# Three small moves in a hybrid mLSTM and attention layer: sample state operations behind the third value tile, sample value rows in idle strips, one gate-up weight piece in tile space of its own

## The chip, the cores and the metric

The kernel runs on one core of one Trainium2 chip, as one launch. The metric is device time in microseconds (us). The engines are TensorE (PE in the profile; its weight loads are PEld), VectorE (DVE), ScalarE (ACT), GpSimd (POOL) and SyncE (SP), which issues nearly all DMA transfers. Each engine works through its own queue in the order in which its instructions stand there, and waits at an instruction until what that instruction needs has been done elsewhere.

## The reference

One inference step of one decoder layer for two groups with the same weights: a prompt of 512 tokens and a sample group of 8 sequences with one token each. All is fp32.

```python
x = layer_norm(x, ln_in_g, ln_in_b)
z = x @ w_in
qk, mv, mi, mf, mo, aq, ak, av, gm, ga = split(z)
qk, conv_state = causal_dwconv(qk, conv_buf, conv_w, conv_b)        # width 4, silu
mq, mk = split(qk, 2)
h, C, n, m = mlstm_chunkwise(mq, mk, mv, mi + b_igate, mf + b_fgate, C0, n0, m0)
h = h * rsqrt(mean(h*h) + RMS_EPS)                                  # per head
y_m = sigmoid(mo) * h * m_norm_g
y_a, k_win, v_win = window_attention(aq, ak, av, k_buf, v_buf, attn_sinks, start)
mixed = sigmoid(gm) * y_m + sigmoid(ga) * y_a
x = layer_norm(ALPHA * x + mixed @ w_out, ln1_g, ln1_b)
g, u = split(x @ w_gate_up, 2)
ffn = (silu(g) * u) @ w_down
ple = sigmoid(x @ w_ple_gate) * (p @ w_ple)
x = layer_norm(ALPHA * x + ffn + ple, ln2_g, ln2_b)
```

The mLSTM has 4 heads with keys of 128 and values of 256 channels. For a sample token, one step of its recurrence is, for each of the 8 sequences and 4 heads,

```python
C_new = decay_prev * C + w_state * outer(k, v)      # 128 x 256 per sequence and head
n_new = decay_prev * n + w_state * k                # 128 per sequence and head
h     = (C_new^T q) / max(|n_new . q|, exp(-m_new))
```

Every C, n and m of the sample group is read, updated and written out. Attention has 16 query and 2 key-value heads of 64 channels and a window of 128.

## The kernel before, in words

Activations are kept transposed, channels on the 128 partitions and 520 columns for the tokens: 8 sample tokens first, then the 512 of the prompt. A projection is worked in tiles `f` of 128 output channels, and each tile in two halves of 264 and 256 columns, one PSUM bank each. fp32 products are made from a high and a low part, with three matmuls for each: high by high, high by low and low by high (L245, which stands for nearly all projection matmuls). So one tile with 1024 input channels is 48 matmuls of L245.

**Weights** come in blocks by DMA (L165, into one of two `raw` buffers) and are used in pieces of 128 x 1024. `prep_next` splits a piece: ACT copies it rounded, the high part (L218, `whi<-raw`), and DVE subtracts, the low part (L219, `wlo<-raw,whi`). The parts go to two rings of three buffers, `whi` and `wlo`, unless `dest` names another place for the piece. `get` splits up to two pieces ahead of the one in use.

**What sets the order.** Outside of `tc.manual_schedule` blocks a scheduler, which simulates the program, sets the order of every engine's queue; code order, dependences and buffer rings are its input. `after(f, ..., f_=[ins])` tells it to issue what `f` makes behind the instruction `ins`. Inside the `manual_schedule` blocks the queues of PE, DVE, POOL and ACT hold what is written, in the written order.

**The projections** run one tile after another, numbered `t`: the mLSTM queries and keys (`qk`, t 0 to 7), its values (`mv`, from `t_mv` = 8), attention keys and values (from `t_k` = 16), attention queries (`aq`, from `t_aq` = 18), and then the gates `mo`, `gm` and `ga`. After each tile `sd.run(t)` takes steps from the lists of side work: `sd.add(steps, start, end)` spreads a list evenly over the tiles from `start` to `end`. All that is neither a projection nor its eviction is side work. The lists that the change touches or borders on are:

- `conv_out` (L967): transposes the last columns of the convolution, copies them from PSUM to `ost` (L973) and stores them (L974, L975). Before, `ost` is a buffer of the ring `stg` with two buffers.
- `ev_mv(f)` (L981) is the eviction of a value tile. ACT copies the two halves into a `stg` buffer (L984), PE transposes that (L987 for the prompt, L992 for the 8 sample rows), DVE copies the results away (L988, L996), and after each second tile the sample rows go to DRAM, to `vsd` (L998).
- `smlstm_prep` (L1095): prepares the sample step. PE transposes the old `n` (L1099); DVE makes the scaled keys `kws` (L1102, L1103), the new `n` (L1104, L1105, in `nst`) and `qn` (L1106); PE transposes `nst` back (L1109), DVE copies that (L1111) and it is stored (L1113). The decay and input factors `wdb` come by a broadcast from DRAM (L913), behind the gate rows `bcd` (L912).
- `ml0` to `ml3`: the prompt's mLSTM in 4 chunks of 128 for each head. `ml0(h)` loads two rows per head, broadcast over the partitions (L1036, L1037), to the strips 2h and 2h+1, POOL adds a mask to the first (L1040); `ml1` reads them chunk by chunk (L1054 on ACT and a product on POOL). A strip is a 128 x 520 tile, and there is one buffer for each of the eight.
- `sm0`, `sm1`, `sm2`: the sample step, in eight units `(h, g)` of one head and four sequences. `sm0` loads the four 128 x 256 matrices `Ct` (L1120) and the four value rows `vb`, broadcast over the partitions from `vsd` (L1121, 512 KB), each to one of four `big` buffers. `sm1` scales the value rows by the keys (ACT, L1141), adds the decayed state (DVE, L1142), splits the result into high and low for the product with the query (L218 on ACT, L219 on POOL), and stores `Ct` (L1152). The units run skewed: in one step of the list the load of one unit, the work of the one before it, and the end (`sm2`) of the one before that.
- attention (`at1` to `at3`: L684 to L743) runs in the same stretch, from `t_aq` on.

**Gate-up.** After the output projection and its LayerNorm the gate and up projections begin. Their first five pieces, `k_gu` to `k_gu+4`, are split before the LayerNorm's last part; a manual block runs their first-half matmuls between the LayerNorm's steps, and their second half after it. Then come pieces 5 to 7, still of the plain kind, and behind them a Strassen phase (L1580 to L1684) that reads combinations of the activations: `tsum` (L1492 to L1496) and `tsplit` (L218, L219 into `tf`) make these on DVE and ACT in the same stretch.

## Time and profile before

| what | value |
| --- | --- |
| time, median of 3 runs | 886.09 us (884.8 to 888.52) |
| time of the profiled execution | 885.6 us |
| its span | 883.5 us |
| mean granted PE clock in it | 0.995 |
| PE busy | 866.0 us (98%) |
| DVE busy | 659.4 us (75%) |
| ACT busy | 475.5 us (54%) |
| POOL busy | 156.2 us (18%) |
| DMA, mean over the span | 117 GB/s |

The span runs from the first instruction to the last that the profiler recorded; the execution's own time has about 2 us more around it. All positions below are microseconds from the span's start. In a row of the timeline stand the start, the busy time, the engine, the line, the operation, the tile that is written and those that are read, how many instructions were put together in the row (x2), and in brackets how long the engine was idle before it and what released it. A row of windows has the stretch, its length, for PE, PEld, DVE, ACT and POOL the busy time and the number of instructions, and then the granted PE clock (1.00 is full speed), the DMA engines' busy share and GB/s. A row of waits has an engine with the line that waited, what released it, the sum in us, how often, and the longest. DMA-issuing queues are called SPq.

### The profile page before, as it was taken

How to read it: one execution, taken by the hardware profiler on the slowest of the kernel's cores; microseconds unless marked ns; L12 is line 12 of the kernel's file. 1: busy time of each engine (PE TensorE's matmuls, PEld its weight loads, DVE VectorE, ACT ScalarE, POOL GpSimd, SP SyncE). 2: the span in 40 equal slices, each digit the busy share in tenths (PEclk: the TensorE clock that was granted, in tenths of full speed). 3: DMA queues.
4: the chain of work that ended last, by engine and by line, in shares of the span. 5: the costliest groups of instructions: out<-in, count | busy, mean ns of one | idle time of the engine just before them, and what ended most of it. 6: DMA issues, size and time to landing. Idle time of an engine off the chain costs nothing.

```text
span 883.5 us, 18583 instructions
## 1 busy us (share of the span) xinstructions
PE 866.0 (98%) x7082; PEld 853.2 (97%) x7082; DVE 659.4 (75%) x1589; ACT 475.5 (54%) x1131; POOL 156.2 (18%) x315
## 2 busy tenths in 40 slices
PE   8999899999999999999999999999999999999996
PEld 7999899999999899999999999999999999999996
DVE  7788555688978676778876968898898875566337
ACT  6545254658777655566525846666666565222120
POOL 5441321115464411221012300000000000000002
PEclk9999999999999999999999999999999999999998
DMA  7642631336465451131520043333334337634212
GB/s 244 223 145 73 194 102 55 55 106 145 157 180 172 145 143 49 49 97 48 191 97 1 23 111 104 112 108 97 107 101 116 108 115 219 202 120 150 96 37 97
DMA packets 125369, 103.69 MB, mean 117 GB/s; under 512 B 7210, under 2 KB 121090, under 8 KB 125256
## 3 DMA queue, kind: packets, MB, share of 16 engines
q1 hardware_dynamic: 125136, 102.38, 38.7%
q8 instruction: 55, 0.90, 0.4%
q14 instruction: 34, 0.28, 0.1%
q10 hardware_dynamic: 144, 0.13, 0.0%
HBM read 91.14 MB, written 12.47 MB: 117 GB/s over the span
## 4 chain that ended last, share of the span: by engine, by line
PE 87%; DVE 5%; DMA 3%; ACT 2%; issue 1%; POOL 1%; SPq 0%; DVEq 0%; ACTq 0%
PE psm L245 41%; PE psm L1601 14%; PE pss L1601 11%; PE psm L228 5%; PE psm L1894 2%; PE psm L1918 2%; PE pss L684 2%; PE pss L737 1%; PE pss L721 1%; PE psm L1429 1%; DMA big<-vsd 1%; PE psm L468 1%; PE pss L1070 1%; PE pss L1074 1%; DMA wdb<-bcd 1%
## 5 line engine op out<-in xcount | busy, mean ns | idle before, releaser
L245 PE MATMUL psm<-T,whi 128*128 128x264 f32 (+1 forms) x1728 | 301.9, 287 | 0.2 <-ACT th L1169 0.2
L245 PEld LDWEIGHTS psm<-T,whi 128*128 128x128 f32 x1728 | 246.8, 189 | 2.1 <-ACT th L1169 0.5
L245 PE MATMUL psm<-T,wlo 128*128 128x256 f32 (+1 forms) x912 | 200.1, 288 | 1.5 <-DVE wlo L219 1.5
L245 PEld LDWEIGHTS psm<-T,wlo 128*128 128x128 f32 x912 | 145.7, 189 | 2.5 <-DVE wlo L219 1.9
L219 DVE TENSOR_TENSOR wlo<-raw,whi 128x1024 fp32r<-128x1024 f32 (+2 forms) x75 | 90.5, 1207 | 66.8 <-ACT whi L218 66.7
L218 ACT ACTIVATE whi<-raw 128x1024 fp32r<-128x1024 f32 (+2 forms) x75 | 77.2, 1034 | 96.9 <-PE psm L245 79.5
L1784 POOL COPY amaskA<-tmp 128x8 f32<-128x8 f32 x8 | 1.5, 189 | 362.9 <-DVE tmp L1782 362.8
L709 POOL TENSOR_SCALAR g<-g,sm 128x256 f32<-128x256 f32 (+1 forms) x64 | 36.2, 579 | 80.2 <-DVE sm L707 23.8
L1585 DVE TENSOR_TENSOR whi<-raw,whi 128x512 fp32r<-128x512 f32 x55 | 37.8, 688 | 11.6 <-ACT whi L1580 10.7
L1580 ACT ACTIVATE whi<-raw 128x512 fp32r<-128x512 f32 x55 | 34.6, 628 | 19.5 <-PE psm L1601 14.4
L1580 ACT ACTIVATE wlo<-raw 128x512 fp32r<-128x512 f32 x55 | 34.6, 629 | 16.3 <-ACT gt L1619 10.2
L1585 DVE TENSOR_TENSOR wlo<-raw,wlo 128x512 fp32r<-128x512 f32 x55 | 37.8, 687 | 6.0 <-ACT wlo L1580 5.6
L702 ACT ACTIVATE g<-g,sm 128x256 f32<-128x256 f32 (+1 forms) x64 | 30.2, 474 | 18.7 <-DVE sm L698 17.7
L245 PE MATMUL psm<-L,whi 128*128 128x264 f32 x192 | 38.7, 282 | 0.0
L219 POOL TENSOR_TENSOR gt<-big,gt 128x256 fp32r<-128x256 f32 x32 | 27.7, 873 | 51.3 <-ACT gt L218 39.5
L1601 PE MATMUL psm<-tf,whi 128*128 128x260 f32 x276 | 36.7, 282 | 0.0
L1601 PE MATMUL psm<-T,wlo 128*128 128x260 f32 x264 | 35.3, 283 | 0.0
L1601 PE MATMUL pss<-tf,whi 128*128 128x260 f32 x264 | 35.3, 283 | 0.0
L1601 PE MATMUL pss<-tf,wlo 128*128 128x260 f32 x264 | 35.3, 283 | 0.0
L1601 PE MATMUL psm<-T,whi 128*128 128x260 f32 x264 | 35.3, 283 | 0.0
L1601 PEld LDWEIGHTS psm<-tf,whi 128*128 128x128 f32 x276 | 34.5, 188 | 0.0
L1601 PE MATMUL psm<-tf,wlo 128*128 128x260 f32 x252 | 33.5, 282 | 0.0
(461 smaller groups left out, 2104.3 us busy)
## 6 DMA issues: line engine op xcount, KB each, us to landing
raw<-in_w_in_dram SPq DMA_DIRECT2D x24, 1024.0 KB
raw<-in_w_gate_up_dram SPq DMA_DIRECT2D x72, 256.0 KB
raw<-in_w_down_dram SPq DMA_DIRECT2D x8, 1024.0 KB
big<-in_state_mlstm_C_dram SPq DMA_DIRECT2D x8, 512.0 KB
big<-vsd SPq DMA_DIRECT2D x8, 512.0 KB
out_dram<-big SPq DMA_DIRECT2D x8, 512.0 KB
raw<-in_w_out_dram SPq DMA_DIRECT2D x4, 1024.0 KB
raw<-in_w_gate_up_dram SPq DMA_DIRECT2D x4, 1024.0 KB
```

The costliest lines, as they stand in the source:

```text
L218: S.activation(rr(hi), src, AF.Copy)
L219: (le or V).tensor_tensor(rr(lo), src, hi, ALU.subtract)
L228: T.matmul(ps[:, :n], rr(w[:, k, wc : wc + P]), rr(a[k0 + k][:, c0 : c0 + n]), start=(i == 0), stop=(i == tot - 1),)
L245: T.matmul(ps[:, :n], rr(w[:, k, wc : wc + P]), rr(a[k0 + k][:, c0 : c0 + n]), start=(i == 0), stop=(i == tot - 1),)
L684: T.matmul(sc[:, a, :w], rr(q[:, a, n * P : (n + 1) * P]), rr(KS[:, kv, hl, (n - 1 + k0) * P : (n + 1) * P]), start=(hl == 0), stop=(hl == 1),
L702: S.activation(pr[:, a, :w], pr[:, a, :w], AF.Exp, bias=sm[:, 2 + a : 3 + a], scale=ASC, accum_out=sm[:, 8 + a : 9 + a],)
L709: G.tensor_scalar(pr[:, a, :w], pr[:, a, :w], sm[:, 12 + a : 13 + a], 0.5, ALU.mult, ALU.mult)
L1580: S.activation(rr(t[:, 0]), wsrcs[i], AF.Copy)
L1585: V.tensor_tensor(rr(lo), wsrcs.pop(i), hi, ALU.subtract)
L1601: T.matmul(ps[:, :TH], rr(w[:, j, :]), rr(x[j]), start=(start and j == 0 and i == 0), stop=(j == 3 and i == 2), skip_group_check=not start,)
L1894: T.matmul(pA[a][:, :264], rr(w[:, a * P : (a + 1) * P]), rr(x[:, :264]), start=(j == 0 and i == 0), stop=(j == KF - 1 and i == 2),)
L1918: T.matmul(pC[c][:, :256], rr(hk[k][x][:, t0 : t0 + P]), rr(w), start=(k == 0 and i == 0), stop=(k == KF - 1 and i == 2),)
```

## The change

1. `conv_out` takes `ost` from the ring `g2` instead of `stg`.
2. `ev_mv` notes its copy of the transposed values (L988). The three steps of `smlstm_prep` are taken at the tiles `t_mv + 2` and `t_mv + 3` instead of `t_mv` to `t_mv + 2`, and are issued behind that copy, which at that time is the one of the third value tile (f = 2).
3. `sm0` no longer puts the value rows into one `big` buffer with one 512 KB broadcast. It loads two halves of 256 KB, one each to the strips 4 + 2g and 5 + 2g, which hold rows of the mLSTM heads 2 and 3 until their last chunk has been worked. `sm1` reads the rows there.
4. Gate-up piece `k_gu+5` gets a place of its own: 1024 columns at the end of slab 3 (`mx3[0]`) for its high part and of `T5[0]` for its low part, both free until the gated activations are written there. Its split is written into the manual block, behind the activation of piece 4's first half.

```diff
@@ conv_out
-            ost = ring("stg", NT, 2)
+            ost = g2()
@@ ev_mv
-        V.tensor_copy(
+        late_t["mv"] = V.tensor_copy(
             vaug()[:, :, f // 2, (f % 2) * P : (f % 2 + 1) * P], ps.rearrange("p (c d) -> p c d", c=NCH)
-        )
+        ).ins
@@ sm0
-        vb = big()[:, :1024].rearrange("p (b d) -> p b d", b=4)
         nc.sync.dma_start(Ct, st_C[0, 4 * g : 4 * g + 4, h].rearrange("b k d -> k b d"))
-        nc.sync.dma_start(
-            vb, vsd[4 * g : 4 * g + 4, h * DV : (h + 1) * DV].partition_broadcast(P)
-        )
+        vb = []
+        for i in range(2):
+            v2 = strip(4 + 2 * g + i)[:, :512].rearrange("p (b d) -> p b d", b=2)
+            b0 = 4 * g + 2 * i
+            nc.sync.dma_start(v2, vsd[b0 : b0 + 2, h * DV : (h + 1) * DV].partition_broadcast(P))
+            vb += [v2[:, 0], v2[:, 1]]
@@ sm1
-            S.activation(vb[:, i, :], vb[:, i, :], AF.Copy, scale=kws[:, h, b : b + 1])
+            S.activation(vb[i], vb[i], AF.Copy, scale=kws[:, h, b : b + 1])
             V.scalar_tensor_tensor(
-                Ct[:, i, :], Ct[:, i, :], wdb[:, h, 1, b : b + 1], vb[:, i, :], ALU.mult, ALU.add
+                Ct[:, i, :], Ct[:, i, :], wdb[:, h, 1, b : b + 1], vb[i], ALU.mult, ALU.add
             )
@@ ev_ga
         if f == 0:
-            mxhi.extend(v3(slab(3)))
+            mx3.append(slab(3))
+            mxhi.extend(v3(mx3[0]))
@@ side work
-    sd.add(gen_steps(smlstm_prep()), t_mv, t_mv + 2)
+    smp = smlstm_prep()
+    sd.add([lambda: after(next, smp, None, f_=[late_t["mv"]]) for _ in range(3)], t_mv + 2, t_mv + 3)
@@ gate-up
     dest[k_gu + 4] = (sub8(T6, 2), sub8(T6, 3))
+    dest[k_gu + 5] = tuple(
+        t[:, 6 * NT : 6 * NT + 1024].rearrange("p (k n) -> p k n", k=KD) for t in (mx3[0], T5[0])
+    )
@@ manual block of gate-up
         ts[4, 0] = ev_g(pg[4], n0)
+        prep_next()
```

Line numbers below are those of the kernel before; in the changed kernel L1141 and L1142 are L1143 and L1144, L1121 is L1124, L1152 is L1154, L1406 is L1414, and L1492 to L1496 are L1501 to L1505.

Three places show what moves in the queues. A number behind a tile's name tells one use of the tile from another, and it differs between the two kernels.

**Place 1, DVE around the value tiles.** `wlo` rows are weight splits; rows from L1102 to L1106 are the first step of `smlstm_prep`. Before:

```order
L219 TENSOR_TENSOR wlo_1405<-raw_1165,whi_1404 128x1024
L1102 TENSOR_TENSOR kws_574<-T_123_603,wdb_570 128x32
L1104 TENSOR_TENSOR nst_575<-pss_1320,wdb_570 128x32
L1103 TENSOR_SCALAR kws_574<-kws_574 128x32
L1105 TENSOR_TENSOR nst_575<-nst_575,kws_574 128x32
L1106 TENSOR_TENSOR qn_576<-nst_575,T_123_603 128x32
L1111 COPY tmp_1329<-pss_1327 32x128
L996 COPY tmp_1298<-pss_1400 8x128
L219 TENSOR_TENSOR wlo_1480<-raw_1165,whi_1479 128x1024
L988 COPY T_195_1231<-pss_1394 128x4x128
L988 COPY T_195_1231<-pss_1461 128x4x128
```

With the change:

```order
L219 TENSOR_TENSOR wlo_1388<-raw_1165,whi_1387 128x1024
L988 COPY T_195_1231<-pss_1377 128x4x128
L996 COPY tmp_1298<-pss_1383 8x128
L219 TENSOR_TENSOR wlo_1480<-raw_1165,whi_1479 128x1024
L996 COPY tmp_1452<-pss_1450 8x128
L988 COPY T_195_1231<-pss_1444 128x4x128
L1102 TENSOR_TENSOR kws_574<-T_123_603,wdb_570 128x32
L1104 TENSOR_TENSOR nst_575<-pss_1456,wdb_570 128x32
L1103 TENSOR_SCALAR kws_574<-kws_574 128x32
L1105 TENSOR_TENSOR nst_575<-nst_575,kws_574 128x32
L1106 TENSOR_TENSOR qn_576<-nst_575,T_123_603 128x32
L219 TENSOR_TENSOR wlo_1587<-raw_1322,whi_1586 128x1024
```

The five operations of `smlstm_prep` stood ahead of the second value tile's rows (L996 and L988 with `pss_1400` and `pss_1394`) and of the next weight split. Now they stand behind the copies of the second and the third value tile (`pss_1377` and `pss_1444`) and behind that split.

On PE the same place reads, before (L245 with `psm_1408` and `psm_1409` is the third value tile, `stg_1391` is the second):

```order
L245 MATMUL psm_1408<-T_19_135,whi_1233 128x264
L245 MATMUL psm_1409<-T_19_135,whi_1233 128x256
L1109 MATMUL pss_1327<-ident_90,nst_575 32x128
L245 MATMUL psm_1408<-T_20_136,whi_1233 128x264
L245 MATMUL psm_1409<-T_20_136,whi_1233 128x256
L245 MATMUL psm_1408<-T_19_135,wlo_1234 128x264
L245 MATMUL psm_1409<-T_19_135,wlo_1234 128x256
L987 MATMUL pss_1394<-ident_90,stg_1391 128x128 x2
```

With the change (`psm_1391` and `psm_1392` are the third value tile here, `stg_1374` is the second):

```order
L245 MATMUL psm_1392<-T_19_135,wlo_1234 128x256
L245 MATMUL psm_1391<-T_19_135,whi_1233 128x264
L987 MATMUL pss_1377<-ident_90,stg_1374 128x128 x4
L992 MATMUL pss_1383<-ident_90,stg_1374 8x128
L245 MATMUL psm_1392<-T_19_135,whi_1233 128x256
L245 MATMUL psm_1391<-T_20_136,whi_1233 128x264
```

The transposes of the second value tile (L987, L992) stood behind the last matmuls of the third tile and behind the transpose of `nst` (L1109). Now they stand 17 matmuls ahead of the third tile's end, and L1109 comes behind the transposes of the third tile (it is row 785 of PE's queue, those are rows 750 to 752; before, it was row 715 and those of the third tile rows 749 and 750).

**Place 2, ACT between the last mLSTM chunks and attention.** `S_..` are strips; L1054 reads the mLSTM rows of a strip, `QSa` is the eviction of an attention query tile. Before:

```order
L1027 ACTIVATE T_123_603<-pss_2375,mgq_542 128x128 x2
L667 ACTIVATE QSa_565<-psm_2557 64x256
L1015 ACTIVATE g_2365,hs_2367<-g_2365,hs_2367 128x256
L1005 ACTIVATE g_2458<-pss_2452 128x257
L1054 ACTIVATE g_2476<-S_282_1788,colI_566 128x128
L1015 ACTIVATE g_2458,hs_2460<-g_2458,hs_2460 128x256
L218 ACTIVATE whi_2951<-raw_2242 128x1024
L667 ACTIVATE QSa_565<-psm_2768 64x256
```

With the change:

```order
L667 ACTIVATE QSa_565<-psm_2559 64x256
L1143 ACTIVATE S_406_2506<-S_406_2506,kws_574 128x256 x2
L1015 ACTIVATE g_2365,hs_2367<-g_2365,hs_2367 128x256
L1005 ACTIVATE g_2458<-pss_2452 128x257
L1054 ACTIVATE g_2476<-S_282_1788,colI_566 128x128
L218 ACTIVATE gt_2668<-big_2504 128x256
L218 ACTIVATE gt_2676<-big_2504 128x256
L1015 ACTIVATE g_2458,hs_2460<-g_2458,hs_2460 128x256
L1143 ACTIVATE S_460_2839<-S_460_2839,kws_574 128x256 x2
L1143 ACTIVATE S_427_2643<-S_427_2643,kws_574 128x256 x2
L218 ACTIVATE whi_2957<-raw_2242 128x1024
L667 ACTIVATE QSa_565<-psm_2772 64x256
```

Six scalings of value rows (three rows of x2, from strips 4, 4 again and 6) and two splits of `big_2504` now stand ahead of the weight split (`whi_2957`; `whi_2951` before). Before, the next scalings of value rows stood 24 rows behind it, and four had been done earlier, at 113.6. SP's queue has, in the same place, the broadcasts to `S_406`, `S_460` and `S_427` one behind the other, ahead of the load of the weight block `raw_2961`; before, the load of that block (`raw_2955`) stood there alone.

**Place 3, DVE in the gate-up stretch.** `wlo_7107` is the low part of piece 5 before; with the change it is the row `L_5613<-raw_6718,T_907_5673`. Before:

```order
L219 TENSOR_TENSOR L_5597<-tmp_6928,T_899_5657 128x264
L1496 SCALAR_TENSOR_TENSOR T_123_603<-T_123_603 128x260
L219 TENSOR_TENSOR tf_7050<-T_123_603,tf_7048 128x260
L219 TENSOR_TENSOR tf_7049<-T_123_603,tf_7047 128x260
L1496 SCALAR_TENSOR_TENSOR T_123_603<-T_123_603 128x260
L219 TENSOR_TENSOR tf_7049<-T_123_603,tf_7047 128x260
L219 TENSOR_TENSOR wlo_7107<-raw_6702,whi_7106 128x1024
```

With the change:

```order
L219 TENSOR_TENSOR L_5613<-tmp_6944,T_907_5673 128x264
L1505 SCALAR_TENSOR_TENSOR T_123_603<-T_123_603 128x260
L219 TENSOR_TENSOR L_5613<-raw_6718,T_907_5673 128x1024
L1505 SCALAR_TENSOR_TENSOR T_123_603<-T_123_603 128x260
L219 TENSOR_TENSOR tf_7073<-T_123_603,tf_7071 128x260
L219 TENSOR_TENSOR tf_7072<-T_123_603,tf_7070 128x260 x2
L219 TENSOR_TENSOR wlo_7130<-raw_6726,whi_7129 128x1024
```

Piece 5's low part has moved ahead of four rows of the activation combinations (L1496, now L1505, and `tf`). On ACT its high part has moved from behind three conversions (`tf`) to the place right behind piece 4's activation (L1406, now L1414), ahead of them.

1 line of the change is left out of this document (added).

## The prediction

> **What bounds the kernel now.** I read the page's busy times and slices first.
>
> ```profile
> PE 866.0 (98%) x7082; PEld 853.2 (97%) x7082; DVE 659.4 (75%) x1589; ACT 475.5 (54%) x1131; POOL 156.2 (18%) x315
> PEclk9999999999999999999999999999999999999998
> PE 87%; DVE 5%; DMA 3%; ACT 2%; issue 1%; POOL 1%; SPq 0%; DVEq 0%; ACTq 0%
> ```
>
> PE is busy 98% of the span at nearly full clock, and it is 87% of the chain of waits (the last row). No matmul of size goes away in the change, so all that can be won is the 883.5 − 866.0 = 17.5 us in which PE stands still, plus stretches in which it is "busy" but slow. The list of PE's waits says where:
>
> ```profile
> PE pss L1109 <- DVE nst L1105: 2.4, 1, 2.4
> PE psm L245 <- DVE wlo L219: 1.5, 1, 1.5
> PE pss L737 <- ACT T L1027: 1.5, 1, 1.5
> ```
>
> These three single waits are at three places that the edits touch: L1109 the sample state's transpose (edits 1 and 2), L737 in attention behind the sample step (edit 3), L245 behind a weight's low part (edit 4). What each costs with what surrounds it is read from windows at those places:
>
> ```profile
> 98.45:100.64 2.19, 2.19 (x19) 1.98 (x17) 1.23 (x1) 0.53 (x1) 0.40 (x1) 1.00 0.70 234
> 100.64:103.08 2.44, 0.00 (x0) 0.03 (x1) 0.71 (x5) 0.57 (x2) 0.00 (x0) 1.00 0.38 143
> 103.08:106.44 3.36, 3.36 (x17) 3.28 (x18) 2.06 (x5) 1.70 (x4) 2.13 (x3) 0.55 0.69 171
> 296.00:302.00 6.00, 4.30 (x34) 3.79 (x33) 5.04 (x12) 4.60 (x12) 2.46 (x3) 1.00 0.68 238
> 308.00:314.00 6.00, 6.00 (x52) 5.83 (x52) 5.12 (x19) 4.18 (x14) 1.12 (x3) 1.00 0.40 111
> ```
>
> At 101 PE stands 2.44 us, and in the 3.36 us behind it the clock is 0.55 and only 17 matmuls run. At the rate of the window ahead (19 in 2.19) 3.36 us hold 29. So the stretch costs 2.44 + 12 × 0.115 = about 3.9 us (the slow part by clock alone: 3.36 × 0.45 = 1.5). At 296 PE does 34 matmuls in 6 us instead of 52, 18 × 0.115 = 2.1 us, and the clock stays at 1.00. The third wait is looked at with its own rows below.
>
> The Trainium skill ("TensorE: Matmul & The Clock Gate", Part 1: The HAM clock gate) asks to keep gaps under about 3 us and gives an idle window of some 3.4 us before the clock falls. This trace has it fall after 2.44 us. By the page the slow 1.5 us would not belong to the wait and would stay when the wait goes, and the sum below would end 1.5 us higher; the rows put the slow stretch right behind the wait, so I count it.
>
> **Edits 1 and 2, around 101.**
>
> ```profile
> 95.47 6.74 DMA wdb<-bcd
> 102.30 0.19 DVE L1102 TENSOR_TENSOR kws<-T,wdb 128x32 f32<-128x32 f32 x1 [2.06 <-DMA wdb<-bcd]
> 103.08 0.27 PE L1109 MATMUL pss<-ident,nst 128*32 128x128 f32 x1 [2.45 <-DVE nst L1105]
> 102.51 0.66 ACT L984 ACTIVATE stg<-psm 128x264 f32<-128x264 f32 x2 [3.52 <-DVE kws L1102]
> 93.05 5.80 POOL L1040 TENSOR_TENSOR S<-S,amaskA 128x128 f32<-128x128 f32 x12 [9.83 <-DVE big L962]
> 97.63 0.40 ACT L1054 ACTIVATE g<-S,colI 128x128 f32<-128x128 f32 x1 [3.15 <-POOL S L1040]
> 97.94 1.04 ACT L218 ACTIVATE whi<-raw 128x1024 fp32r<-128x1024 f32 x1
> 98.79 0.64 PE L245 MATMUL psm<-T,whi 128*128 128x264 f32 x4
> ```
>
> The broadcast `wdb` lands at 102.2, DVE waits for it at L1102, and PE stands behind DVE. Second, ACT's eviction of value tile 2 (L984) began at 102.51 only. DVE is named as its releaser, but L1102 gives it nothing; what it lacked was a `stg` buffer, since both were held by the convolution's last columns until their stores. With edit 1 those are in `g2`, with edit 2 L1102 and L1109 stand behind value tile 3. In the new order PE reaches the transposes of tile 2 (L987) 17 matmuls ahead of tile 3's end. L1109 stood 4 ahead of it, so that is the row 13 matmuls ahead of the old wait, the second of the four that begin at 98.79: about 98.9. The eviction it needs stands on ACT behind L1054 and the weight split, which ends at 97.94 + 1.04 = 98.98; with 0.66 for the two halves, 99.65. So a wait stays there, 99.65 − 98.9 = **0.75 us**, too short for the clock by the wait of 1.5 us at 298 that left it at 1.00. Behind it, L1102 is reached after tile 3's copy, some 50 matmuls (5.7 us) later, near 105, when `wdb` has been there for 2 us; L1105 needs four operations of 0.19 more, and PE is at L1109 about 35 rows × 0.115 = 4 us after tile 3's transposes. DVE hides all of it. Gain 3.9 − 0.75 = **3.15 us**; ends 0 (the new wait as long as the old) and 3.9.
>
> **Edit 3, gain around 298.**
>
> ```profile
> 288.17 8.17 DMA big<-vsd
> 296.42 1.71 ACT L1141 ACTIVATE big<-big,kws 128x256 f32<-128x256 f32 x4 [5.37 <-DMA big<-vsd]
> 296.96 1.28 DVE L1142 SCALAR_TENSOR_TENSOR big<-big,wdb,big 128x256 f32<-128x256 f32 x3 [5.01 <-ACT big L1141]
> 298.49 0.51 PE L737 MATMUL pss<-big,VS 128*128 128x256 f32 x2 [1.48 <-ACT T L1027]
> ```
>
> The last unit's value rows could be asked for only when a `big` buffer came free, at 288.17, and took 8.17 us. ACT stood 5.37 us for them, with attention's work queued behind. In strips the rows of a unit are asked for as soon as the scaled rows of the unit two before it have been added (L1142), several us earlier, and two `big` buffers more are free for `Ct`. The ACT wait should vanish, and PE's 2.1 us with it. **2.2 us** (with 0.1 for short waits up to 302); ends 0 (if `Ct`, behind a store for its buffer, comes as late) and 3.5, by the row of the longer stretch, which has 161 matmuls where the rate of 308 to 314 gives 191: 30 × 0.115.
>
> ```profile
> 287.14:309.23 22.09, 20.23 (x161) 19.01 (x160) 15.10 (x45) 14.06 (x41) 10.24 (x15) 1.00 0.46 145
> ```
>
> **Edit 3, price around 185 to 230.**
>
> ```profile
> 184.02 0.39 ACT L1054 ACTIVATE g<-S,colI 128x128 f32<-128x128 f32 x1
> 186.51 0.38 ACT L667 ACTIVATE QSa<-psm 64x256 fp32r<-64x256 f32 x1
> 191.44 1.06 ACT L218 ACTIVATE whi<-raw 128x1024 fp32r<-128x1024 f32 x1 [0.56 <-PE psm L245]
> 216.84 1.04 ACT L218 ACTIVATE whi<-raw 128x1024 fp32r<-128x1024 f32 x1
> 89.64 1.32 SPq L1036 DMA_DIRECT2D S<-bcd  x3
> 217.85 0.37 SPq L1121 DMA_DIRECT2D big<-vsd  x1
> 223.88 0.51 ACT L1141 ACTIVATE big<-big,kws 128x256 f32<-128x256 f32 x1 [1.76 <-DMA big<-vsd]
> 202.99 0.27 PE L721 MATMUL pss<-ident,g 128*128 128x128 f32 x1
> 190.00:196.00 6.00, 6.00 (x48) 5.84 (x47) 4.88 (x15) 4.00 (x12) 0.55 (x1) 1.00 0.13 26
> 196.00:203.00 7.00, 7.00 (x61) 7.00 (x61) 5.15 (x24) 4.44 (x17) 3.02 (x5) 1.00 1.14 249
> sum 45.00, PE 45.00 PEld 44.11 DVE 37.47 ACT 32.49 POOL 16.00; mean PE 6.43 PEld 6.30 DVE 5.35 ACT 4.64 POOL 2.29
> ```
>
> Between 184 and 229 PE has no idle time (45.00 of 45.00 in the last row), and ACT has 12.5 us. Up to the weight split at 216.84 the old order has four scalings there, the new one fourteen: ten more of 0.43 (four in 1.71, above) and their splits, some 6 us, ahead of evictions of attention's queries. They also wait. `S_406` can be asked for when ACT's L1054 has read the strip (184.4), and ACT comes to it after L667 at 186.9. `S_460` goes to the same strip and is asked for only behind the addition of `S_406`, and the next weight split stands behind it. How long a 256 KB broadcast takes, no row shows. The nearest is the 260 KB one of the mLSTM rows: issued at 89.64, read by POOL at 93.05, so 3.4 us at most. The other bound is the 512 KB one: 217.85 to 223.88, 6.0 us. I take 3.4, the nearest size. Then `S_406` is there at 187.8 (ACT 0.9 us late), scaled and added at 189.9, `S_460` at 193.3; with four scalings (1.7) the weight split starts at 195.0 instead of 191.44. ACT is idle for 2.0 and 2.56 us in the two windows from 190 to 203; that takes up nearly all of these 3.5 us, though not all of it stands ahead of the same reader, so that PE at L721 (202.99) loses some 0.3. The scalings of `S_461`, `S_428` and `S_492` then come ahead of the evictions at 209 to 222, which I put 1 to 2 us late. My value is **2.0 us** lost; ends 0 (ACT's idle time takes all) and 4.5 (all that is late is felt once more at 216.84).
>
> **Edit 4, around 503.**
>
> ```profile
> 505.02 0.39 PE L245 MATMUL psm<-T,wlo 128*128 128x264 f32 x1 [1.52 <-DVE wlo L219]
> 498.76 0.37 ACT L1406 ACTIVATE gt<-psm 128x264 f32<-128x264 f32 x1
> 500.86 1.05 ACT L218 ACTIVATE whi<-raw 128x1024 fp32r<-128x1024 f32 x1
> 502.06 0.42 DVE L1496 SCALAR_TENSOR_TENSOR T<-T 128x260 f32<-128x260 f32 x1
> 503.76 1.21 DVE L219 TENSOR_TENSOR wlo<-raw,whi 128x1024 fp32r<-128x1024 f32 x1
> ```
>
> PE comes to piece 5's low part at 505.02 − 1.52 = 503.5. It was made from 503.76 on, with DVE full. Now ACT's high part stands right behind L1406 (499.1 to 500.1) and DVE's low part behind the addition at 502.06: 502.4 to 503.6. PE then waits 0.15. The four rows that it passes are combinations for the Strassen phase, read after 520, and DVE has idle time before that. Gain 1.52 − 0.15 = **1.37**; ends 0 (a late ACT in front of it) and 1.52.
>
> **Sum,** against the profiled execution: 885.6 − 3.15 − 2.2 − 1.37 + 2.0 = 880.9. The median of the runs shown (886.09) is 0.5 above that execution, so 880.9 to 881.4: **881.2 us**.
>
> **The rivals.**
>
> *No price (R1).* ACT's 12.5 us of idle time take all of the new work: 885.6 − 6.72 = **878.9**. For it: the other engines wait for ACT seldom there. Against: PE has no slack between 184 and 229, and ACT's order puts 3.5 us of late work right ahead of PE's food.
>
> *The wait moves to the strips (R2, the other side).* The place is ACT's queue from 187 to 200, with weight split, evictions and attention's softmax behind `S_460`. If a half broadcast takes 6.0 us, as the whole one, `S_406` is there at 190.4, `S_460` at 198.5, the split starts at 200.2 and is 9 us late, not 3.5. ACT's 4.6 us of gaps don't hold the additional 5.2 beside the first 3.5, so PE loses 2.0 + 5.2, and over 2.44 us of standing the clock falls too (1.5): 885.6 − 6.72 + 8.7 = **887.6**. It comes out slower than before once the price is over 6.7, that is at 3.4 + 4.7 / 2 = 5.75 us for a half, since two in a row count. For it: the 512 KB ones above took 6.0 and 8.2 us, and I don't know that size sets it. Against: the 3.4 us of a like one.
>
> *The first wait only changes its name (R3).* L987 of tile 2 waits for ACT, and ACT's L1054 ahead of it for POOL's 5.80 us of L1040. If POOL is 1.7 us later, PE stands 2.4 us again with the slow clock behind it: edits 1 and 2 win nothing, and **884.0** is left. Against: nothing ahead of POOL moves.
>
> **How the numbers follow.** The forecast 0.52 (its own range 878.5 to 884), R1 0.22, R2 0.11, R3 0.15. Less than 0.5% (4.43 us) is about what a measurement of this kernel can't tell from no change, so faster is under 881.66, slower over 890.5. Faster: a bit over half of the forecast's cases and R1, 0.30 + 0.21 = 0.51. Slower: the upper part of R2 and what I have not seen, 0.07. The same: 0.42. The range takes in R1 with the whole of the first gain (878.1), less 1 us for noise, and R3 with edit 3 giving 2 less: **877 to 886.5**.
>
> **What would show it.** In the new profile PE's waits should have no L1109 and no 1.5 us at `wlo`, but up to 0.75 us at L987 behind ACT's L984; the clock near 103 should be 1.00; the gap of ACT before the last unit's scalings should be gone and the slice at 287 hold about 180 matmuls. Between 187 and 230 PE should show 1 to 3 us of short waits, behind attention's tiles or `QSa`. A half broadcast over 5 us, or a PE wait over 2.4 us there, would make the forecast wrong, and so would a wait at `Ct` in place of the value rows.

## The result, and the profile after

The changed kernel takes 894.89 us (median of 6 runs, 892.15 to 899.02), the kernel before 885.74 us in the runs beside it. The ratio is **1.0103** (95% interval 1.0067 to 1.0139): the change is slower by 9 us, where 881.2 us were forecast, faster by 5. The profiled execution took 896.29 us, its span 894.5.

The page of the kernel after, its busy times and clock, and its list of PE's waits:

```profile
PE 868.7 (97%) x7082; PEld 855.7 (96%) x7082; DVE 661.6 (74%) x1589; ACT 475.0 (53%) x1131; POOL 158.2 (18%) x315
PEclk9999999999999999999999999999999999999999
```

```profile
PE pss L1150 <- ACT g L1005: 3.8, 1, 3.8
PE pss L1150 <- ACT gt L218: 3.3, 1, 3.3
...
PE pss L987 <- ACT stg L984: 1.4, 1, 1.4
...
PE psm L245 <- DVE wlo L219: 0.4, 1, 0.4
PE psm L245 <- DVE L L219: 0.2, 1, 0.2
```

The three waits at which the edits were aimed have gone or shrunk: no L1109, 0.2 and 0.4 us at a weight's low part instead of 1.5, no L737. In their place stand two large waits at L1150, the product of the new sample state with the query (L1148 before), which had no wait before.

To see where time is won and lost, I counted PE's matmuls in windows of 2 us, and took for each count the time at which it is reached. (A matmul that reaches over the edge of a window counts in both, in every kernel alike.) The difference to the kernel before, in us:

| count of matmuls | time before | after | e1 no strips | e3 prep alone | e5 in unit order | e9 no n store | e6 head 0 in big | e13 order, no n |
| --- | --- | --- | --- | --- | --- | --- | --- | --- |
| 800 | 93.6 | +2.3 | +2.3 | +3.2 | -0.3 | +2.2 | +0.3 | +0.4 |
| 900 | 108.2 | 0.0 | -0.1 | +0.7 | -2.7 | -0.2 | -2.1 | -2.1 |
| 1100 | 130.2 | 0.0 | +1.2 | +2.6 | -2.9 | -0.4 | -2.0 | -2.2 |
| 1700 | 198.9 | -0.6 | +0.6 | +2.6 | -3.1 | -0.4 | -2.4 | -2.7 |
| 2100 | 241.1 | +12.2 | +0.9 | +4.1 | +7.9 | +4.4 | -1.7 | -1.8 |
| 2600 | 294.5 | +11.7 | +0.2 | +3.6 | +7.2 | +7.8 | -2.4 | -2.2 |
| 2700 | 307.5 | +10.4 | -0.5 | +2.2 | +4.5 | +5.1 | -4.9 | -4.6 |
| 4500 | 498.4 | +10.5 | -0.6 | +2.1 | +3.5 | +5.0 | -5.3 | -5.0 |
| 4700 | 521.3 | +9.1 | -2.1 | +2.2 | +2.0 | +3.5 | -6.7 | -6.4 |
| 5900 | 647.7 | +8.7 | -2.5 | +2.3 | +1.7 | +3.0 | -6.7 | -6.8 |

What stands in the row of 800 came about before any edit; it differs by up to 3.5 us between these executions, so the steps between rows are read, not the rows. For the change they are: **2.3 us won** around 101, 0.6 more by 199, **12.8 us lost** between 199 and 241, **1.3 won** around 300 (1.8 with the slower gain ahead of it) and **1.4 won** around 503.

The loss in windows of the two kernels, before and then after:

```profile
195.00:250.00 55.00, 55.00 (x458) 54.20 (x456) 47.30 (x154) 42.50 (x126) 25.75 (x48) 1.00 0.60 164
```

```profile
195.00:250.00 55.00, 45.88 (x353) 43.65 (x353) 38.27 (x123) 37.55 (x110) 19.40 (x39) 0.97 0.67 154
...
212.29:218.00 5.71, 5.71 (x36) 5.69 (x37) 5.42 (x16) 4.50 (x12) 2.53 (x4) 0.70 1.28 215
```

In 55 us PE does 353 matmuls in place of 458, 105 × 0.12 = 12.6 us. 9.1 us of it PE stands. Of the rest, 1.6 us is a slow clock: behind the first large wait it is 0.70 for 5.7 us, with 36 matmuls where about 49 would fit. The timeline of the kernel after, by engine (ACT, then SP's issues, then PE):

```profile
188.18 0.91 ACT L1143 ACTIVATE S<-S,kws 128x256 f32<-128x256 f32 x2 [0.76 <-DMA S<-vsd]
193.38 1.71 ACT L1143 ACTIVATE S<-S,kws 128x256 f32<-128x256 f32 x4 [1.99 <-DMA S<-vsd]
209.54 0.91 ACT L1143 ACTIVATE S<-S,kws 128x256 f32<-128x256 f32 x2 [4.41 <-DMA S<-vsd]
223.95 0.91 ACT L1143 ACTIVATE S<-S,kws 128x256 f32<-128x256 f32 x2 [4.58 <-DMA S<-vsd]
...
185.01 5.93 SPq L1124 DMA_DIRECT2D S<-vsd  x3
197.32 0.37 SPq L165 DMA_DIRECT2D raw<-in_w_in_dram  x1
199.03 1.36 SPq L1085 DMA_DIRECT2D out_dram<-Cst  x1
200.48 0.41 SPq L1124 DMA_DIRECT2D S<-vsd  x1
...
213.50 0.42 SPq L1085 DMA_DIRECT2D out_dram<-Cst  x1
214.02 1.54 SPq L1124 DMA_DIRECT2D S<-vsd  x2
...
212.29 0.78 PE L1150 MATMUL pss<-gt,qz 128*40 128x256 f32 x5 [3.81 <-ACT g L1005]
225.21 0.31 PE L1150 MATMUL pss<-gt,qz 128*40 128x256 f32 x1 [3.34 <-ACT gt L218]
```

The first three half broadcasts (issued from 185.01 on) are there at 188.18 and 193.38, as forecast, and the weight split behind them begins at 194.99, where 195.0 was worked out. The fourth, the second half of the first unit, is issued at 200.48 and lands at 209.54: 9.1 us. A later one is issued at 214.02 and lands at 223.95: 9.9 us. ACT stands 4.41 and 4.58 us for them, and behind each scaling the sum and its split must follow before PE's L1150. And though PE has projection matmuls in its queue that need none of this, L1150 stands ahead of them in it. Over the whole kernel ACT's waits for the value rows have grown, from the first row (before) to the second (after):

```profile
ACT big L1141 <- DMA big<-vsd: 11.9, 7, 5.4
```

```profile
ACT S L1143 <- DMA S<-vsd: 18.2, 10, 4.6
```

The sum alone decides nothing: e1 and e15 below have 19.1 and 18.0 us of such waits, and neither is slower than the kernel before by more than 0.2%. It matters where a wait stands and what stands behind it.

The two transfers are not late for want of bandwidth. Windows of the kernel after, ahead of the two landings:

```profile
204.00:209.50 5.50, 4.48 (x33) 4.00 (x31) 1.97 (x4) 1.12 (x2) 2.52 (x4) 1.00 0.61 74
218.00:222.00 4.00, 3.87 (x33) 3.65 (x31) 3.67 (x10) 1.32 (x4) 1.32 (x1) 1.00 0.55 14
```

The engines of DMA move 74 and 14 GB/s there, with 164 in mean over the stretch in the kernel before, and yet they count as busy for 0.61 and 0.55 of the time. So something other than the amount of data holds them up. Both late broadcasts were issued right behind L1085, the store of the prompt's new n for one head: a column of 128 partitions with 4 bytes each.

### The profile page after: what moved, and what is told of

Read it like the earlier page. It is cut to its first block, busy times and chain, and to the rows that moved or that the text cites. A ratio compares the mean times of both kernels' runs of the same rounds, so it can differ in the third digit from the quotient of the medians.

```text
span 894.5 us, 18603 instructions
## 1 busy us (share of the span) xinstructions
PE 868.7 (97%) x7082; PEld 855.7 (96%) x7082; DVE 661.6 (74%) x1589; ACT 475.0 (53%) x1131; POOL 158.2 (18%) x315
## 4 chain that ended last, share of the span: by engine, by line
PE 63%; DVE 4%; ACT 2%; DMA 1%; issue 1%; POOL 0%; DVEq 0%; ACTq 0%
PE psm L245 25%; PE psm L1610 14%; PE pss L1610 10%; PE psm L228 5%; PE psm L1903 2%; PE psm L1927 2%; PE pss L684 1%; PE pss L737 1%; PE psm L1437 1%; PE pss L721 1%; DMA raw<-in_w_down_dram 1%; ACT T L1380 1%; DMA big<-in_state_mlstm_C_dram 1%; DVE big L1144 1%; ACT T L1388 1%
## 5 line engine op out<-in xcount | busy, mean ns | idle before, releaser
L245 PE MATMUL psm<-T,whi 128*128 128x264 f32 (+1 forms) x1696 | 295.3, 287 | 1.2 <-DVE Qbd L671 1.2
L245 PEld LDWEIGHTS psm<-T,whi 128*128 128x128 f32 x1696 | 241.3, 189 | 2.9 <-PE psm L245 1.6
L245 PE MATMUL psm<-T,wlo 128*128 128x264 f32 (+1 forms) x896 | 194.1, 288 | 0.4 <-DVE wlo L219 0.4
L245 PEld LDWEIGHTS psm<-T,wlo 128*128 128x128 f32 x896 | 142.3, 189 | 1.4 <-DVE wlo L219 0.6
L219 DVE TENSOR_TENSOR wlo<-raw,whi 128x1024 fp32r<-128x1024 f32 (+1 forms) x74 | 89.8, 1215 | 71.1 <-ACT whi L218 71.0
L218 ACT ACTIVATE whi<-raw 128x1024 fp32r<-128x1024 f32 (+1 forms) x74 | 76.1, 1033 | 98.1 <-PE psm L245 80.9
L709 POOL TENSOR_SCALAR g<-g,sm 128x256 f32<-128x256 f32 (+1 forms) x64 | 36.4, 581 | 92.1 <-DVE sm L707 27.7
L245 PE MATMUL psm<-L,whi 128*128 128x264 f32 x192 | 38.8, 282 | 0.0
```

Source lines behind the costliest of these rows:

```text
L218: S.activation(rr(hi), src, AF.Copy)
L219: (le or V).tensor_tensor(rr(lo), src, hi, ALU.subtract)
L245: T.matmul(ps[:, :n], rr(w[:, k, wc : wc + P]), rr(a[k0 + k][:, c0 : c0 + n]), start=(i == 0), stop=(i == tot - 1),)
L709: G.tensor_scalar(pr[:, a, :w], pr[:, a, :w], sm[:, 12 + a : 13 + a], 0.5, ALU.mult, ALU.mult)
```

## The experiments

### Which edit loses: e1 to e4

**e1** is the change without its third edit:

```diff
+        vb = big()[:, :1024].rearrange("p (b d) -> p b d", b=4)
         nc.sync.dma_start(Ct, st_C[0, 4 * g : 4 * g + 4, h].rearrange("b k d -> k b d"))
-        vb = []
-        for i in range(2):
-            v2 = strip(4 + 2 * g + i)[:, :512].rearrange("p (b d) -> p b d", b=2)
-            ...
+        nc.sync.dma_start(vb, vsd[4 * g : 4 * g + 4, h * DV : (h + 1) * DV].partition_broadcast(P))
```

> The change without its third edit: the value rows go to a big buffer again in one 512 KB broadcast; the other edits stay. Theory 1 (the whole loss comes from the strips: ACT stands 4.41 us and 4.58 us for half broadcasts at 209.5 and 224, and PE behind it): PE keeps up with the kernel before between 180 and 250, the wait of 5.37 us of ACT at 296 is back, and the sum is 2.3 won around 101 and 1.5 around 503: 3.8 us under the kernel before, ratio 0.9957. Rival (the other edits shift the scheduler's order and have a part in the loss between 200 and 250): PE loses some of its 12 us there, and the time is 0 to 8 us over before.

Measured: 883.52 us, ratio 0.9982 (0.9967 to 0.9998). **e2** has that edit alone:

> Only the third edit: value rows in the strips, two broadcasts of 256 KB for a unit. Theory 1: 12 us lost between 200 and 250, 1.8 won near 298, so 10 us over before, ratio 1.012. Rival (the loss needs the moved sample preparation too, which delays the sample state's inputs): 0 to 4 us over before.

Measured: 895.67 us, ratio 1.0116 (1.0096 to 1.0137). So the third edit costs the whole loss, and needs no other edit for it. **e3** is the first and the second edit alone:

> Only the first and second edit: the convolution's last columns in g2, sample preparation behind the third value tile. Theory 1: 2.3 us won around 101, with a wait of some 1.4 us left at L987 behind the eviction on ACT, nothing else moves: ratio 0.9974. The rival of the first expectation: part of the loss between 200 and 250 shows here, ratio above 1.000.

Measured: 883.95 us, ratio 0.9983 (0.9969 to 0.9997). **e4** is the fourth edit alone:

> Only the fourth edit: gate-up piece 5 in a place of its own, split in the manual block. Both theories: 1.1 to 1.5 us won at 503, ratio 0.9985; if the freed raw buffer or the moved split only shifts the wait to pieces 6 and 7, ratio 1.000 and a wait of over 1 us behind 510.

Measured: 883.9 us, ratio 0.9985 (0.9971 to 1.0000), as expected.

e1 and e3 won less than expected, 0.0018 and 0.0017 in place of 0.0043 and 0.0026. The table shows where: they win 2.4 to 2.5 us around 101 and lose 1.3 to 1.9 again by the count of 1100. The timeline of e1 there:

```profile
115.05 1.71 ACT L1141 ACTIVATE big<-big,kws 128x256 f32<-128x256 f32 x4 [7.83 <-DMA big<-vsd]
...
118.04 0.71 PE L987 MATMUL pss<-ident,stg 128*128 128x128 f32 x4 [1.00 <-ACT stg L984]
```

With the preparation moved, the scheduler puts the first unit's scaling of value rows three rows further ahead in ACT's queue, before the next weight split and the fourth value tile's eviction; ACT stands 7.83 us for the 512 KB broadcast, and PE 1.0 us behind it. In the whole change the rows are in strips that are not free at that time, so that this wait can't arise. The edits are not independent.

### What the strips do: e5 to e8

**e5** keeps the whole change and ties the scalings of a unit to the end of the unit before it on ACT:

```diff
+        prev = late_t["sma"]
         for i in range(4):
             b = 4 * g + i
-            S.activation(vb[i], vb[i], AF.Copy, scale=kws[:, h, b : b + 1])
+            with tc.issue_after(prev):
+                S.activation(vb[i], vb[i], AF.Copy, scale=kws[:, h, b : b + 1])
             ...
-            split(cc[0], cc[1], Ct[:, i, :], G)
+            late_t["sma"] = S.activation(rr(cc[0]), Ct[:, i, :], AF.Copy).ins
+            G.tensor_tensor(rr(cc[1]), Ct[:, i, :], cc[0], ALU.subtract)
```

(For the first unit `sma` is the last value tile's eviction.)

> The whole change, with one more constraint: on ACT the scalings of a unit's value rows stand behind the last split of the unit before it, so none is done ahead of its turn (in the change those of unit (1,0) stand ahead of half of unit (0,0)'s). The strips and the broadcasts stay. Theory 1 (the loss comes from half broadcasts that land some 9 us after their issue, because they are queued behind a weight block of 1 MB and beside a state load; the second half of unit (0,0) is one of them): ACT still stands about 4 us at that scaling near 209, and half of the 12 us stays: ratio 1.002 to 1.006. Theory 2 (the loss is the scalings taken ahead of their turn, which load ACT and its queue): it goes, ratio 0.994 to 0.997.

Measured: 890.41 us, ratio 1.0052 (1.0032 to 1.0072): half of the loss against the kernel before stays, as theory 1 had it, but mostly not at the place that it named. Nor is the other half won back there: by the table e5 still loses 11.0 us between the counts of 1700 and 2100, the change 12.8. What else it wins over the change it wins around 300 (1.4 us more) and from there to 498 (1.1). At the first unit ACT stands 3.59 us and PE 1.31 us; the large wait is at the second unit's second half, which is again issued right behind L1085. Timeline of e5, SP's issues, ACT, PE:

```profile
208.44 0.42 SPq L1085 DMA_DIRECT2D out_dram<-Cst  x1
208.96 0.38 SPq L1124 DMA_DIRECT2D S<-vsd  x1
...
217.91 0.91 ACT L1145 ACTIVATE S<-S,kws 128x256 f32<-128x256 f32 x2 [5.48 <-DMA S<-vsd]
...
221.50 0.43 PE L1153 MATMUL pss<-gt,qz 128*40 128x256 f32 x1 [5.65 <-ACT gt L1150]
```

No weight block was issued in the 17 us ahead of 208.96, and the transfer takes 9.0 us.

**e6** is e5 with the two units of head 0 in big buffers, the way the kernel before had them (`if h >= 1:` strips, `else:` one 512 KB broadcast to `big()`):

> As e5, but the two units of head 0 keep their value rows in a big buffer with one broadcast, as in the kernel before; heads 1 to 3 have them in the strips. On ACT the order is then that of the kernel before up to the second unit, and every strip's broadcast has a unit's time (15 us or more) to land. Theory 1: no wait near 209 and 224, the wait of 5.4 us near 296 is gone, and the sums around 101 and 503 are kept: 2.3 + 1.5 + 1.8 = 5.6 us under before, ratio 0.9937. Rival (strips as such cost, by sixteen small broadcasts in the queues or by single buffers): ratio above 1.000, with waits behind 220.

Measured: 880.71 us, ratio **0.9943** (0.9928 to 0.9959). All three gains are there and nothing is lost between 195 and 250 (table). The same stretch of e6, 2 us earlier by what it has won:

```profile
193.00:248.00 55.00, 54.65 (x453) 53.71 (x452) 46.35 (x152) 42.22 (x125) 23.34 (x48) 1.00 0.61 169
```

453 matmuls, with 458 before and 353 after. So the strips of heads 1 to 3 cost nothing as such; what strips cost in the change is a matter of which broadcast stands where in the queues. **e7** has the units of heads 0 and 1 in big buffers:

> As e6, with the units of heads 0 and 1 in big buffers and those of heads 2 and 3 in the strips. Theory 1: the same 5.6 us under before, ratio 0.9937, and the first 270 us as in the kernel before but for the wait at 101. If the queue of DMA is crowded by requests for the strips at 185, a new wait of some 1 us shows near 200.

Measured: 880.74 us, ratio 0.9947 (0.9930 to 0.9964). The crowded queue that was named as a risk shows, in its timeline of SP's issue and ACT's wait:

```profile
195.72 0.51 SPq L1129 DMA_DIRECT2D big<-vsd  x1
...
210.81 1.71 ACT L1152 ACTIVATE big<-big,kws 128x256 f32<-128x256 f32 x4 [4.92 <-DMA big<-vsd]
```

That broadcast took 15 us, and PE waits 2.2 us at its product; nevertheless the median is e6's, within the intervals. (The profiled execution, 883.45 us, is the slowest of e7's six, so the trace may show more waiting than most of them have.) **e8** is the whole change with the half broadcasts issued by POOL (`nc.gpsimd.dma_start` in place of `nc.sync.dma_start`):

> The whole change, with the half broadcasts issued by POOL instead of SP, so that they no longer stand in one queue behind weight loads and stores. Theory 1 in the form that it is the place in SP's queue: the broadcast of the second half of unit (0,0) is issued some 10 us earlier, ACT's wait near 209 is gone, ratio 0.996. Theory 1 in the form that the transfers share the DMA engines with the weight block: it is issued earlier and lands late all the same, ratio 1.005 or more. POOL's queue, which has little to do there, may itself hold the issue behind its own waits: then the waits move and the ratio is above 1.005 too.

Measured: 903.94 us, ratio 1.0205 (1.0180 to 1.0229). By its time the test is inconclusive on the queue, since POOL's own queue got in the way, as feared. Its wait list has a new first row:

```profile
PE pss L721 <- POOL g L709: 7.5, 4, 4.7
```

POOL waits in order until a strip is free before it can issue, and attention's multiplications (L709) stand behind that. The trace of e8 does tell something of the queue. Two of its half broadcasts are issued, in POOL's queue, within 0.1 us of a store of n in SP's queue, and they too are late. The second of them, with the store and ACT's scaling:

```profile
218.83 0.76 POOL L1124 DMA_DIRECT2D S<-vsd  x1 [5.60 <-DVE T L669]
218.86 0.42 SPq L1085 DMA_DIRECT2D out_dram<-Cst  x1
...
229.97 1.70 ACT L1143 ACTIVATE S<-S,kws 128x256 f32<-128x256 f32 x4 [3.37 <-DMA S<-vsd]
```

That is 11.1 us. The trace also records when each of a transfer's 16 pieces is complete. By the last of them the two took 7.9 and 11.1 us and one that was issued 4.2 us behind a store 7.4; the other thirteen took 3.6 to 6.9 us. So a place in another queue doesn't spare a broadcast: what counts is that the store is on its way at the same time.

### What makes the broadcasts late: e9 to e14

**e9** leaves out the store of n, one line of `ml2`:

```diff
             nc.sync.dma_start(o_Cp[0, 0, h], C[:, :DV])
-            nc.sync.dma_start(o_np[0, 0, h].unsqueeze(1), C[:, DV : DV + 1], allow_slow_non_contiguous=True)
```

> The whole change without the four stores of the prompt's n (L1085: a column of 128 partitions with 4 bytes each; this kernel leaves that output out). The queues are else in the order of the change. Two half broadcasts land late in the change, and both were issued right behind such a store (199.03 and 213.50), while the engines of DMA moved only 53 to 72 GB/s and 9 to 31 GB/s before they landed; the three issued before the first store landed in about 3 us. Theory 3 (the small store holds up what is queued behind it): both broadcasts land 3 to 5 us after their issue, ACT's waits of 4.41 and 4.58 us are gone or under 2 us, and most of the 12 us is back: ratio 0.995 to 0.999. Theory 1 as told so far (the weight block of 1 MB ahead and the state load beside it): no difference, ratio 1.010.

Measured: 890.21 us, ratio 1.0052 (1.0034 to 1.0071). Timeline of e9, the issue and the scaling of the half that came at 209.54 in the change:

```profile
199.44 0.96 SPq L1123 DMA_DIRECT2D S<-vsd  x1
...
205.14 0.89 ACT L1142 ACTIVATE S<-S,kws 128x256 f32<-128x256 f32 x2
```

The weight block is ahead of it as in the change, but it is there by 205.14 without a wait of ACT: 5.7 us at most, not 9.1. So the weight block alone does not make it late. But the queues are not else those of the change, as the expectation has it: without the store the scheduler set another order from about 200 on, and the state load that the change issues 0.5 us behind this broadcast (200.94) comes at 208.02 here. So e9 doesn't single out the store; e13 does, below. The other late one goes too: ACT's longest wait for value rows is 2.6 us. But the expectation of theory 3 was 0.995 to 0.999, and half of the loss against the kernel before is still there; in the stretch from the count of 1700 to 2600 it is 8.2 us of the change's 12.3. What is left are ACT's waits for halves that were asked for only just before, ten of them and 15.0 us in all, with the row of PE behind the longest of them:

```profile
ACT S L1142 <- DMA S<-vsd: 15.0, 10, 2.6
...
257.22 0.31 PE L1149 MATMUL pss<-gt,qz 128*40 128x256 f32 x1 [2.23 <-ACT gt L218]
```

Behind that pause the clock is slow again (last table), so this one place (from the count of 2150 to that of 2250) costs about 3.6 us of the 8.2.

**e10** stores n as four rows of 512 bytes instead, so that nothing is left out:

```diff
+    npc = t1([P, MH], "npc")
 ...
-            nc.sync.dma_start(o_np[0, 0, h].unsqueeze(1), C[:, DV : DV + 1], allow_slow_non_contiguous=True)
+            G.tensor_copy(npc[:, h : h + 1], C[:, DV : DV + 1])
+            if h == MH - 1:
+                pt = pss()
+                T.transpose(pt[:MH, :P], npc, ident)
+                npr = ring("tmp", 264, 4)
+                V.tensor_copy(npr[:MH, :P], pt[:MH, :P])
+                nc.sync.dma_start(o_np[0, 0], npr[:MH, :P])
```

> The whole change, with the prompt's n collected as four columns of one tile, transposed on PE after the last head and stored as four rows of 512 bytes. Nothing is left out. Theory 3: as e9, ratio 0.995 to 0.999. Theory 1: ratio 1.010.

Measured: 887.56 us, ratio 1.0021 (1.0008 to 1.0034), between the two expectations. **e11** puts that into e6, **e12** into the kernel before:

> e6 (head 0's value rows in big buffers, scalings in the order of the units) with n stored as rows as in e10. Theory 3: e6 had no wait left at a broadcast, so the time is that of e6, ratio 0.994, with less scatter. Theory 1: the same.

> The kernel before with n stored as rows, none of the four edits. Theory 3: the 512 KB broadcast issued at 196.73, behind two of these stores, lands about 5 us earlier than 208.53, but ACT waited for it only 0.77 us, so the time stays: ratio 0.998 to 1.000.

Measured: e11 882.12 us, ratio 0.9965 (0.9951 to 0.9979), no better than e6; e12 891.91 us, ratio **1.0071** (1.0053 to 1.0090), slower than before where no change was expected. By the count of matmuls e12 loses 2.1 us around 240, and 5.1 us between 390 and 440, at a place where nothing was edited; its longest new wait is PE's L228 behind ACT, 2.5 us (2.9 in two). A transpose and some copies let the scheduler set another order there, which I did not follow further; e10 and e14 can hold such a shift too. On the landing e12 came out as expected: the 512 KB broadcast that took 11.8 us in the kernel before took 7.4.

e5 and e9 each gave half of the loss against the kernel before back. **e13** does both, **e14** the same with n stored as rows (e5 and e10):

> e5 and e9 together: the whole change with all value rows in strips, scalings in the order of the units, and without the stores of the prompt's n (that output is left out). Theory (two causes that add up: broadcasts late behind the small store, which e9 took away, and scalings ahead of their turn, which e5 took away; each gave about half of the loss back): no loss is left between 195 and 250, ratio 0.994 to 0.997. Rival (one cause, of which each of the two runs took away the same half; what remains is the strips themselves): ratio 1.003 to 1.005.

> The same with nothing left out: e5 with n stored as four rows of 512 bytes behind the last head. Theory of two causes: ratio 0.994 to 0.998. Rival: 1.001 or more (e10 alone had 1.0021).

Measured: e13 882.23 us, ratio 0.9961 (0.9947 to 0.9976); e14 880.89 us, ratio **0.9948** (0.9927 to 0.9968). The rival of one cause is out: with both taken away nothing is left of the loss, and there is no third cause of a size that shows. ACT's waits for value rows in e13, the stretch, and the issue and the scaling of the half that took 9.0 us in e5:

```profile
ACT S L1144 <- DMA S<-vsd: 1.7, 3, 1.0
...
192.50:247.50 55.00, 54.54 (x451) 53.30 (x451) 48.17 (x156) 44.26 (x129) 26.24 (x49) 1.00 0.60 186
...
205.81 0.39 SPq L1123 DMA_DIRECT2D S<-vsd  x1
...
209.71 0.91 ACT L1144 ACTIVATE S<-S,kws 128x256 f32<-128x256 f32 x2 [0.45 <-DMA S<-vsd]
```

e5 and e13 are the clean pair for the store. Their traces have the same instructions in the same order on PE and POOL, one instruction in another place on ACT and on DVE each, and the same transfers in the same order but for the four stores. The ratio goes from 1.0052 to 0.9961, so in that order the stores of n cost 8 us. From issue to the last completed piece, in us:

| transfer | with stores of n | without |
| --- | --- | --- |
| second half of the first unit, 256 KB | after 9.0, e5 7.9 | e9 5.4, e13 5.0 |
| half issued behind the next head's stores, 256 KB | after 9.9, e5 8.9 | e9 3.8, e13 3.9 |
| store of C just ahead of the first of these, 128 KB | after 10.6, e5 8.5 | e9 5.2, e13 4.8 |

The last row shows that the store of n also delays what was issued 0.4 us ahead of it.

The two causes do not simply add up. Between the counts of 1700 and 2600 the change loses 12.3 us, e5 10.3, e9 8.2 and e13 none (0.5): taking away one of them gives back 2 and 4 us, taking away both all of it. Either alone keeps most of the loss. (These are single executions; the times, 4.5 and 4.7 us for the one or the other and 12.7 for both, say the same less sharply.)

### Which part of the first gain is whose: e15

**e15** is the second edit alone (`ost` stays in the ring `stg`):

> The second edit without the first: sample preparation behind the third value tile, the convolution's last columns still in the two stg buffers. If the eviction of the second value tile (L984) waits for a stg buffer, as the prediction read it, ACT still begins it at about 102.5 of the kernel before, PE waits about 2 us at L987 in place of L1109, and the ratio is 0.999 to 1.001. If that eviction had waited for DVE's L1102, as the profile names it, the gain is that of both edits, 0.998.

Measured: 886.57 us, ratio 1.0014 (1.0002 to 1.0025): no gain. Timeline of e15, ACT and PE:

```profile
102.83 0.67 ACT L984 ACTIVATE stg<-psm 128x264 f32<-128x264 f32 x2 [3.95 <-DMA out_dram<-stg]
...
103.28 0.69 PE L987 MATMUL pss<-ident,stg 128*128 128x128 f32 x2 [2.64 <-ACT stg L984]
```

The eviction waits for the stores to leave a `stg` buffer, now by name, and PE waits for it at L987, 2.64 us, about as long as it had waited at L1109 (2.45). The buffer was a second wait right behind the first.

## Why the prediction was wrong, point by point

**Edits 1 and 2: right in kind, a quarter less in size.** 3.15 us were forecast, 2.3 won. The reading that the eviction lacked a `stg` buffer, against the profile's releaser L1102, was right (e15). The wait that was to stay at L987 was put at 0.75 us and is 1.43. The timeline of the kernel after, POOL, ACT, PE:

```profile
96.00 6.63 POOL L1040 TENSOR_TENSOR S<-S,amaskA 128x128 f32<-128x128 f32 x12 [9.80 <-DVE big L962]
...
101.43 0.40 ACT L1054 ACTIVATE g<-S,colI 128x128 f32<-128x128 f32 x1 [4.44 <-POOL S L1040]
...
103.11 0.71 PE L987 MATMUL pss<-ident,stg 128*128 128x128 f32 x4 [1.43 <-ACT stg L984]
```

POOL's twelve additions took 6.63 us, 5.80 before, and began some 0.7 us later against the rest of the program (96.00 − 93.05, less the 2.3 by which all is late there). So POOL is 1.5 us late, nearly the 1.7 of the third rival; but PE comes to L987 half a microsecond later than worked out too, and what is left, 1.43, did not bring the slow clock. That clock went with the old wait. By the rule of the Trainium skill ("TensorE: Matmul & The Clock Gate", Part 1: The HAM clock gate), as the prediction told it, it would have stayed; this trace decides for counting it. In part that is luck: in e12, which has none of the four edits, PE stands 2.16 us at this place and the clock stays at 1.00 (last table).

**Edit 3, gain at 298: right, by e6 and e13.** 2.2 us were forecast, 2.5 and 2.4 won there from the count of 2600 to 2700. The change itself has 1.3 to 1.8, but that doesn't show the gain: PE is 11.7 us late by then, and e3, without strips and 3.6 us late, has no wait at L737 either and wins 1.4 there. The kernel after has 52 matmuls in 296 to 302 and loses a few in the next window:

```profile
296.00:302.00 6.00, 6.00 (x52) 6.00 (x52) 5.66 (x14) 2.47 (x8) 2.62 (x2) 1.00 0.50 150
302.00:308.00 6.00, 5.21 (x42) 4.70 (x41) 4.07 (x12) 3.85 (x12) 4.46 (x7) 1.00 0.08 27
```

**Edit 4: right.** 1.37 forecast, 1.4 measured; the wait that is left was put at 0.15 us and is 0.17:

```profile
515.57 0.39 PE L245 MATMUL psm<-T,L 128*128 128x264 f32 x1 [0.17 <-DVE L L219]
```

**Edit 3, price: the step that failed.** 2.0 us were forecast, 12.8 measured, and the upper end of 4.5 didn't hold it. Two things in that step were wrong.

First, "How long a 256 KB broadcast takes ... I take 3.4, the nearest size." The size was not what mattered. The three halves whose landing the step worked out (188, 193) did land in 3.1 to 3.5 us; I then did no such working for the later ones and only put the evictions "1 to 2 us late". The rows for it were in the trace of before:

```profile
195.64 0.46 SPq L1085 DMA_DIRECT2D out_dram<-Cst  x1
196.73 0.62 SPq L1121 DMA_DIRECT2D big<-vsd  x1
...
208.53 1.71 ACT L1141 ACTIVATE big<-big,kws 128x256 f32<-128x256 f32 x4 [0.77 <-DMA big<-vsd]
```

The big broadcast that was issued 1.1 us behind one of the same small stores was used 11.8 us later. (e12's expectation speaks of two stores; the other was issued at 206.07.) I had left it out as one of another size. It cost ACT only 0.77 us there, since the order of before gave it the time. The bound should have come from the transfer beside the same small store, not from one of like size in a quiet stretch.

Second, behind the first three halves the price of the scalings ahead of their turn was counted as ACT's busy time (ten times 0.43 us) against ACT's 12.5 us of idle time. Without the store of n this order alone still costs 8 us (e9 against e13, where ACT waits for value rows 1.7 us in all in place of 15.0), not as busy time but because ACT then stands at data that was asked for just before, and holds back all that is behind it. Idle time of an engine with one queue is no reserve when its new work has to wait.

The second rival had the right queue and the right side: the wait moves to ACT's queue behind the strips, at 887.6 us and a chance of 0.11. Its mechanism was off, since it made the first halves slow and those were fast; and it priced one stretch of waits where there were two. Its condition, a half that takes over 5.75 us, was met by the two that it did not speak of. The prediction had also named the two signs that would make it wrong, a half broadcast over 5 us and a PE wait over 2.4 us; both came.

**Ends and chances.** The range ended at 886.5; the term that failed had no row of its own for either of its two causes, and its upper end was drawn from the same wrong landing time.

## What to carry to other kernels

A transfer's time to land depends on what else is on its way, from other queues too; take it from a transfer that had the same neighbours, and look at the GB/s of the last microseconds: if they are low while the engines of DMA count as busy, as here beside the 4-byte stores, the amount of data is not what holds it up. When a scheduler moves work to the front because its simulated transfer is early, look in the new order for instructions of a one-queue engine that wait for a load issued only just before, and ask what stands behind them. And before a wait is called removed, ask for a second resource that the same instruction lacks at the same time (here a buffer behind an operand): each alone wins nothing.

When two causes are taken away one at a time, the rest may look like half of each; only the run without both, and a pair that differs in one thing alone (here e5 and e13), tells what each is worth.

Two versions that keep all four edits in essence and leave nothing out are faster than both kernels: e6, with head 0's rows in big buffers and the scalings in the order of the units, at 0.9943 of the time before (0.9928 to 0.9959), and e14 at 0.9948 (0.9927 to 0.9968).
